# Two triangles of sliding-window scores merged into one matrix before the softmax and parted after the transpose

## The chip, the cores and the metric

The kernel runs on one core of a Trainium2 chip. The metric is the device time of one execution in microseconds; beside it stands a profile of one execution, in which times count from the first instruction. TensorE is PE in the rows (PEld are its weight loads), VectorE is DVE, ScalarE is ACT, GpSimd is POOL, and SP issues most of the transfers.

## The reference, cut to what matters

The reference is one inference step of a decoder layer with two branches: a retention branch and a sliding-window attention branch with learned sinks, 16 query heads in 4 groups of 4, head size 64, window 128. Only the second branch for the prompt (1024 tokens, 8 blocks of 128) is touched:

```python
i = arange(128)[:, None]; j = arange(256)[None, :]
d = i + 128 - j
band = (d >= 0) & (d < 128)             # keys of the block before, and of this one
s = q k^T * HD**-0.5, -inf outside band # 128 queries x 256 keys
p = softmax(concat([s, sink]))[..., :-1]
o = p v
```

For query i, the allowed keys of the block before are those with j > i, and those of its own block are those with j <= i. The two sets are complementary triangles of a 128x128 square. Block 0 has no block before it.

## The kernel before

Work is in three phases; all of the change lies in the first, which projects the normalised tokens and runs both branches. Every fp32 product is done with operands split into a high part (rounded to the fast matmul type, by ScalarE) and a low part (the rest, by a subtract on VectorE or GpSimd): `copy_hi_lo` at L138. The weights are split by `load_unit`, L151 to L170, ScalarE for the high part (L168) and GpSimd for the low part (L169), up to six units at a time and two units ahead of their use.

Phase one goes through eight groups: four heads of retention, then four key groups of the sliding window (4 query heads each). Each group goes over eight tiles of 128 tokens. A tile of the sliding window (`swa_tile`) has five parts, and the loop in `groups` interleaves those of neighbouring tiles with blocks of gate and merge projections (`gate_block`, `mg_block`: 24 matmuls of 344 columns each):

1. projection of 384 columns (24 matmuls), rotary and norm, in which GpSimd raises the mean squares to the power -0.5 (`rstd`, L147);
2. transposes of queries and keys (L512, L513) and their splits;
3. scores: for each of four heads two matmuls of 256 columns (L532, L533) into PSUM; then VectorE adds the band mask, scales by the query's norm and takes the row maximum in one instruction per head (L536), writing 128x256 to `s`; then `softmax_tail`: exponentials on ScalarE (L486), and a scaling by 1/sum per head on VectorE (L491);
4. for both key blocks: four transposes of `s` on TensorE into one PSUM tile (L546), high part on ScalarE, low part on VectorE (L549, both in the helper's lines L139 and L140);
5. for both key blocks two matmuls of 512 columns with the split values (L556, L557).

Tiles with t = 0 have one key block only. The decode rows (`swa_rows`) use the same `softmax_tail` with one head and 128 keys.

The order of instructions on each engine is not the program's: a planner (L984, `schedule_with_timeline_sim=True`) walks the program with durations of its own and, for each engine, writes down the instructions as they become ready, earlier program parts first. At run time each engine keeps to that order and waits on semaphores. Buffers are limited: three accumulators in PSUM for projections, two tiles for transposes (`ptr`), two for scores (`psc`), one for the product with the values (`pav`).

Of the kernel before, what the change touches and what calls it, by code (L numbers as in the profile page):

```python
# [8 lines left out]

F32 = mybir.dt.float32  # L10
F32R = mybir.dt.float32r
AF = mybir.ActivationFunctionType
ALU = mybir.AluOpType
AX = mybir.AxisListType
# [3 lines left out]
P = 128  # L18
# [9 lines left out]
SH, KVH, G, HD = 16, 4, 4, 64  # L28
WIN = 128
# [3 lines left out]
NEG = -1e30  # L33
# [38 lines left out]
def shape_constants():  # L72
    c, s = rope_tables(DK)
    out = {}
    cols = SEQ + NS
    ct = np.concatenate([c[:cols].T, c[:cols].T], 0)
    st = np.concatenate([s[:cols].T, -s[:cols].T], 0)
    out["c_ropeT"] = np.stack([ct, st], 1)
    tm = np.concatenate([c, s], 1).reshape(NT + 1, P, 128)
    tm[NT] *= DK ** -0.5  # L80
    out["c_ropeK"] = tm.transpose(1, 0, 2)
    c2, s2 = rope_tables(HD)
    tm = np.concatenate([c2, s2], 1).reshape(NT + 1, P, HD)
    out["c_ropeS"] = tm.transpose(1, 0, 2)
    lg = log_decay()
    m = np.arange(P)[:, None]
    n = np.arange(P)[None, :]
    sc = DK ** -0.5
    out["c_maskT"] = np.stack([(n >= m) * np.exp(-(m + 1.0) * lg[h]) * sc for h in range(RH)], 1)
    i = np.arange(P)[:, None]  # L90
    j = np.arange(2 * P)[None, :]
    d = i + P - j
    out["c_band"] = np.where((d >= 0) & (d < WIN), 0.0, NEG)
    misc = np.zeros((P, 8 + 8 + 64 + 128 + 8))
    for h in range(RH):
        misc[:, h] = np.exp((np.arange(P) + 1.0) * lg[h])
        misc[:, 4 + h] = np.exp((P - 1.0 - np.arange(P)) * lg[h]) * sc
    for r in (0, 32, 64):
        misc[r : r + 8, 8:16] = np.eye(8)
    misc[:, 16:80] = np.eye(8).reshape(1, 64)  # L100
    z = np.zeros((2, HD, NS // 2, NS, G))
    for b in range(NS):
        z[b % 2, :, b // 2, b, :] = 1.0
    misc[:, 80:208] = z.reshape(P, 128)
    for r in range(NS * G):
        misc[r, 208 + r // G] = 1.0
    out["c_misc"] = misc
    return {k: np.ascontiguousarray(v.astype(np.float32)) for k, v in out.items()}
# [14 lines left out]
class Body:  # L123
# [27 lines left out]
    def load_unit(self, spec):  # L151
# [3 lines left out]
        raw = self.t(self.wp, [P, D], "wraw", bufs=RAW)  # L155
        hi = self.t(self.wp, [P, D], "whi", F32R, bufs=self.wbufs)
        lo = self.t(self.wp, [P, D], "wlo", F32R, bufs=self.wbufs)
        view = lambda x: x[:, : nk * width].rearrange("p (k c) -> p k c", k=nk)
# [81 lines left out]
    def norm_h(self, t):  # L240
# [16 lines left out]
        else:  # L257
            junk = self.t(self.ap, [NS, NS, DK], "zk", F32R, bufs=1)[:]
        ss = self.t(self.sm, [P, 1], "ss", bufs=4)
# [82 lines left out]
    def ret_tile(self, h, t, units, qT, st, oT):  # L342
# [4 lines left out]
        self.rope_k(kr[:], acc[:, :DK], t)  # L347
        vhi = self.t(self.ap, [P, DV], "vhi", F32R, bufs=3)
        vlo = self.t(self.ap, [P, DV], "vlo", F32R, bufs=3)
# [124 lines left out]
        nc.vector.tensor_scalar(out=kd[:p], in0=kr[:p].broadcast_to([p, 2, HD]), scalar1=rs[:, 4:5], scalar2=None, op0=ALU.mult)  # L474
        return qr, kd, rs

    def softmax_tail(self, s, mx, nsink, sink, p, nh, nk):
        nc = self.nc
        ng = self.t(self.sm, [P, 4], "ng", bufs=2)
        ds = self.t(self.sm, [P, 4], "ds", bufs=2)  # L480
        l = self.t(self.sm, [P, 4], "l", bufs=2)
        r = self.t(self.sm, [P, 4], "r", bufs=2)
        nc.vector.scalar_tensor_tensor(out=ng[:p, :nh], in0=mx, scalar=-1.0, in1=nsink, op0=ALU.mult, op1=ALU.min)  # L483
        nc.vector.tensor_tensor(out=ds[:p, :nh], in0=sink, in1=ng[:p, :nh], op=ALU.add)
        for j in range(nh):
            nc.scalar.activation(out=s[:p, j, :nk], in_=s[:p, j, :nk], func=AF.Exp, bias=ng[:p, j : j + 1], accum_out=l[:p, j : j + 1])  # L486
        nc.scalar.activation(out=ds[:p, :nh], in_=ds[:p, :nh], func=AF.Exp)
        nc.vector.tensor_tensor(out=l[:p, :nh], in0=l[:p, :nh], in1=ds[:p, :nh], op=ALU.add)
        nc.vector.reciprocal(out=r[:p, :nh], in_=l[:p, :nh])
        for j in range(nh):  # L490
            nc.vector.tensor_scalar(out=s[:p, j, :nk], in0=s[:p, j, :nk], scalar1=r[:p, j : j + 1], scalar2=None, op0=ALU.mult)  # L491

    def swa_tile(self, g, t, units, st, oT):
        nc = self.nc
        acc = self.t(self.pacc, [P, 512], "acc")
        self.gemm_tok(acc[:, :384], units, self.hhi, self.hlo, t)
        qr, kd, rs = self.swa_rope(acc[:, :384], t)
# [12 lines left out]
        pt = self.t(self.ptr, [P, 4, P], "tr")  # L510
# [4 lines left out]
        for a in range(2):  # L515
            src = pt[a * HD : (a + 1) * HD, 0:2, :]
# [5 lines left out]
        yield  # L522
        k0 = (t - 1) * P if t else 0
        nk = 2 * P if t else P
        band = self.band[:, 2 * P - nk :]
        s = self.t(self.ap, [P, G, 2 * P], "s", bufs=2)
        mx = self.t(self.sm, [P, 4], "mx", bufs=2)
        for i in range(2):
            sc = self.t(self.psc, [P, 2, 256], "sc")
            for a in range(2):  # L530
                j = 2 * i + a
                nc.tensor.matmul(sc[:, a, :nk], qs[:, i, a, :], khi[:, k0 : k0 + nk], start=True, stop=False)  # L532
                nc.tensor.matmul(sc[:, a, :nk], qs[:, i, a, :], klo[:, k0 : k0 + nk], start=False, stop=True)  # L533
            for a in range(2):
                j = 2 * i + a
                nc.vector.tensor_tensor_reduce(  # L536
                    out=s[:, j, :nk], in0=sc[:, a, :nk], in1=band, scale=rs[:, j : j + 1], scalar=-3e38,
                    op0=ALU.add, op1=ALU.max, accum_out=mx[:, j : j + 1])
        self.softmax_tail(s, mx[:], self.nsink[:, G * g : G * g + G], self.sink[:, G * g : G * g + G], P, G, nk)
        yield  # L540
        nblk = nk // P
        pT = []
        for blk in range(nblk):
            pt = self.t(self.ptr, [P, 4, P], "tr")
            for j in range(G):
                nc.tensor.transpose(out=pt[:, j, :], in_=s[:, j, blk * P : (blk + 1) * P], identity=self.ident[:])  # L546
            hi = self.t(self.ap, [P, 512], "pThi", F32R, bufs=2)
            lo = self.t(self.ap, [P, 512], "pTlo", F32R, bufs=2)
            self.copy_hi_lo(hi[:], lo[:], pt[:].rearrange("p a b -> p (a b)"), nc.vector)  # L549
            pT.append((hi, lo))  # L550
        yield
        vs = [vprev, vv] if nblk == 2 else [vv]
        po = self.t(self.pav, [P, 512], "av")
# [11 lines left out]
    def swa_rows(self, g, units, oT):  # L565
        nc = self.nc
# [5 lines left out]
        qr, kd, rs = self.swa_rope(kv[:], NT, NS)  # L572
# [8 lines left out]
        pt = self.t(self.ptr, [P, 512], "tr")  # L581
# [5 lines left out]
        pt = self.t(self.ptr, [P, 512], "tr")  # L587
# [8 lines left out]
        R = NS * G  # L596
        sc = self.t(self.psc, [P, 512], "sc")
        for i in range(NS // 2):
            nc.tensor.matmul(sc[:R, :P], zq[:, i].rearrange("p a b -> p (a b)"), kcT[:, i * P : (i + 1) * P], start=(i == 0), stop=(i == NS // 2 - 1))
        s = self.t(self.ap, [R, 1, P], "srow", bufs=1)  # L600
        mx = self.t(self.sm, [P, 4], "mx", bufs=2)
        nc.vector.tensor_copy(out=s[:, 0, :], in_=sc[:R, :P])
        nc.vector.tensor_reduce(out=mx[:R, 0:1], in_=s[:, 0, :], axis=AX.X, op=ALU.max)
        self.softmax_tail(s, mx[:R, 0:1], self.nsinkr[:, g : g + 1], self.sinkr[:, g : g + 1], R, 1, P)
        yield
        pt = self.t(self.ptr, [P, 512], "tr")
        nc.tensor.transpose(out=pt[:, :R], in_=s[:, 0, :], identity=self.ident[:R, :R])
# [10 lines left out]
        pt = self.t(self.ptr, [P, 512], "tr")  # L618
# [226 lines left out]
    def swa_consts(self):  # L845
        nc, ap = self.nc, self.ap
        self.cK = self.t(ap, [P, NS, KVH * HD], "cK")
        self.cV = self.t(ap, [P, NS, KVH * HD], "cV")
        self.swa_tables()
        nc.sync.dma_start(out=self.rng[:], in_=self.i["ret_norm_g"][0].rearrange("h (i p) -> p (h i)", p=P))  # L850
        nc.vector.tensor_scalar(out=self.rng[:], in0=self.rng[:], scalar1=0.5, scalar2=None, op0=ALU.mult)
        self.band = self.t(ap, [P, 2 * P], "band")
        nc.sync.dma_start(out=self.band[:], in_=self.i["c_band"][:])
        self.sink = self.t(ap, [P, SH], "sink")
        nc.sync.dma_start(out=self.sink[:], in_=self.i["swa_sinks"][0:1, :].broadcast_to([P, SH]))
        self.nsink = self.t(ap, [P, SH], "nsink")
        nc.vector.tensor_scalar(out=self.nsink[:], in0=self.sink[:], scalar1=-1.0, scalar2=None, op0=ALU.mult)
        self.sinkr = self.t(ap, [NS * G, KVH], "sinkr")
        for b in range(NS):
            nc.sync.dma_start(out=self.sinkr[b * G : (b + 1) * G, :], in_=self.i["swa_sinks"][0].rearrange("(g j) -> j g", g=KVH))  # L860
        self.nsinkr = self.t(ap, [NS * G, KVH], "nsinkr")
        nc.vector.tensor_scalar(out=self.nsinkr[:], in0=self.sinkr[:], scalar1=-1.0, scalar2=None, op0=ALU.mult)
        for dst, name in ((self.cK, "cache_swa_k"), (self.cV, "cache_swa_v")):
            nc.sync.dma_start(out=dst[:], in_=self.i[name][0].rearrange("b k g d -> k b (g d)"))
# [123 lines left out]
```

## Time and profile before

| | |
|---|---|
| median of 3 runs | 1203.67 us (1202.83 to 1205.09) |
| profiled execution, its own time | 1204.67 us |
| its span, first to last instruction | 1202.9 us |
| mean granted clock of TensorE | 0.997 of full speed |
| busy: TensorE, VectorE, ScalarE, GpSimd | 1180.1, 671.3, 456.7, 355.4 us |

Matmuls overlap in their pipeline, so the duration of one is longer than the distance to the next; what one more matmul costs is read from the starts of neighbours. Idle time of an engine counts only if TensorE in the end waits for it.

### The profile page before, as it was taken

The numbers are of one execution on the slowest core, as the hardware profiler recorded it, in microseconds if no ns is written. First come the engines' busy times: TensorE is split into PE (matmuls) and PEld (weight loads), VectorE is DVE, ScalarE is ACT, GpSimd is POOL, SyncE is SP. The second block draws the span as 40 slices with busy tenths as digits, with TensorE's granted clock in tenths as the row PEclk, the third lists the DMA queues.
The fourth block names the chain that finished last, engine by engine and source line by source line (L and its number), as shares of the span: only waits on it lengthen the run. The fifth ranks groups of instructions, "written<-read, shape, count | busy, mean of one in ns | idle before, by whom it ended". The sixth has DMA issues, their size and how long they took to land.

```text
span 1202.9 us, 19501 instructions
## 1 busy us (share of the span) xinstructions
PE 1180.1 (98%) x7228; PEld 1114.3 (93%) x7228; DVE 671.3 (56%) x2018; ACT 456.7 (38%) x1158; POOL 355.4 (30%) x282
## 2 busy tenths in 40 slices
PE   6999999999999999999999999999999999999998
PEld 5899999999999999999999999999899999999876
DVE  5755545555544477777766777677754421565121
ACT  6543443334334245554454446444544310221010
POOL 5425016216225432422342224122532131221010
PEclk9999999999999999999999999999999999999999
DMA  9124115313113401310141013101526744554221
GB/s 324 51 72 118 55 42 162 112 42 108 51 61 101 139 32 57 109 37 19 44 135 37 8 56 110 55 7 37 172 65 241 230 149 143 166 161 138 78 89 71
DMA packets 125168, 116.71 MB, mean 97 GB/s; under 512 B 17480, under 2 KB 113224, under 8 KB 125040
## 3 DMA queue, kind: packets, MB, share of 16 engines
q1 hardware_dynamic: 118160, 106.99, 28.7%
q10 hardware_dynamic: 6912, 8.46, 2.0%
q8 instruction: 57, 0.93, 0.3%
q14 instruction: 39, 0.32, 0.1%
HBM read 85.05 MB, written 32.44 MB: 98 GB/s over the span
## 4 chain that ended last, share of the span: by engine, by line
PE 93%; DVE 4%; ACT 1%; DMA 1%; issue 1%; POOL 0%; SPq 0%; ACTq 0%
PE acc L212 16%; PE acc L213 16%; PE acc L214 16%; PE acc L223 10%; PE acc L224 10%; PE acc L222 9%; PE tr L546 2%; PE acc L233 1%; PE acc L232 1%; PE av L441 1%; PE sc L532 1%; PE sc L533 1%; PE av L557 1%; DVE s L491 1%; PE av L556 1%; PE tr L339 1%
## 5 line engine op out<-in xcount | busy, mean ns | idle before, releaser
L169 POOL TENSOR_TENSOR wlo<-wraw,whi 128x1024 fp32r<-128x1024 f32 (+1 forms) x92 | 204.9, 2236 | 335.5 <-ACT whi L168 250.1
L212 PE MATMUL acc<-hhi,whi 128*128 128x344 f32 x864 | 281.0, 325 | 0.6 <-ACT tg L298 0.6
L213 PE MATMUL acc<-hlo,whi 128*128 128x344 f32 x864 | 278.8, 323 | 0.0
L214 PE MATMUL acc<-hhi,wlo 128*128 128x344 f32 x864 | 278.3, 322 | 0.0
L222 PE MATMUL acc<-whi,hhi 128*128 128x384 f32 x512 | 175.1, 343 | 2.4 <-ACT hhi L139 1.2
L224 PE MATMUL acc<-whi,hlo 128*128 128x384 f32 x512 | 175.4, 343 | 0.0
L223 PE MATMUL acc<-wlo,hhi 128*128 128x384 f32 x512 | 175.3, 343 | 0.0
L212 PEld LDWEIGHTS acc<-hhi,whi 128*128 128x128 f32 x864 | 162.8, 188 | 2.3 <-ACT tg L298 0.9
L213 PEld LDWEIGHTS acc<-hlo,whi 128*128 128x128 f32 x864 | 162.5, 188 | 1.8 <-issue 1.0
L214 PEld LDWEIGHTS acc<-hhi,wlo 128*128 128x128 f32 x864 | 162.5, 188 | 1.4 <-issue 0.6
L147 POOL TENSOR_TENSOR rs<-ms,nhalf 128x1 f32<-128x1 f32 (+3 forms) x81 | 69.4, 858 | 298.3 <-DVE ms L146 294.1
L168 ACT ACTIVATE whi<-wraw 128x1024 fp32r<-128x1024 f32 (+1 forms) x92 | 90.2, 982 | 163.1 <-PE acc L213 104.5
L222 PEld LDWEIGHTS acc<-whi,hhi 128*128 128x128 f32 x512 | 97.2, 190 | 3.9 <-ACT hhi L139 1.6
L223 PEld LDWEIGHTS acc<-wlo,hhi 128*128 128x128 f32 x512 | 97.5, 190 | 1.5 <-issue 0.8
L224 PEld LDWEIGHTS acc<-whi,hlo 128*128 128x128 f32 x512 | 97.3, 190 | 0.5 <-DVE hlo L140 0.2
L486 ACT ACTIVATE s<-s,ng 128x256 f32<-128x256 f32 (+1 forms) x128 | 61.7, 484 | 27.3 <-DVE ng L483 27.2
L288 POOL TENSOR_TENSOR oT<-oT,tg 128x344 f32<-128x344 f32 x48 | 45.7, 954 | 84.3 <-DVE tg L286 61.6
L536 DVE CUSTOM_DVE_ANT_0 s<-sc,band,rs 128x256 f32<-128x256 f32 (+1 forms) x128 | 53.6, 460 | 17.9 <-PE sc L533 17.7
L139 ACT ACTIVATE pThi<-tr 128x512 fp32r<-128x512 f32 x60 | 35.2, 596 | 52.5 <-PE tr L546 52.1
L140 DVE TENSOR_TENSOR pTlo<-tr,pThi 128x512 fp32r<-128x512 f32 x60 | 41.0, 686 | 21.3 <-ACT pThi L139 20.9
L491 DVE TENSOR_SCALAR s<-s,r 128x256 f32<-128x256 f32 (+1 forms) x128 | 52.1, 468 | 0.7
L224 PE MATMUL acc<-whi,mlo 128*128 128x512 f32 x128 | 50.5, 395 | 0.0
(346 smaller groups left out, 2364.2 us busy)
## 6 DMA issues: line engine op xcount, KB each, us to landing
wraw<-in_w_in SPq DMA_DIRECT2D x36, 512.0 KB
d_t<-tg ACTq DMA_DIRECT2D x48, 172.0 KB
d_o<-oT SPq DMA_DIRECT2D x16, 516.0 KB
tt<-d_t SPq DMA_DIRECT2D x48, 172.0 KB
wraw<-in_w_in SPq DMA_DIRECT2D x32, 256.0 KB
st<-d_o SPq DMA_DIRECT2D x9, 516.0 KB
d_m<-tt SPq DMA_DIRECT2D x24, 172.0 KB
mm<-d_m SPq DMA_DIRECT2D x24, 172.0 KB
```

What stands on the lines that cost most here:

```text
L147: nc.gpsimd.tensor_tensor(out=rs[:p, :width], in0=ms[:p, :width], in1=self.nhalf[:p, :width], op=ALU.pow)
L168: nc.scalar.activation(out=hi[:, :f], in_=raw[:, :f], func=AF.Copy)
L169: nc.gpsimd.tensor_tensor(out=lo[:, :f], in0=raw[:, :f], in1=hi[:, :f].bitcast(F32), op=ALU.subtract)
L212: nc.tensor.matmul(ps, whi[:, k, :], hi[:, cs], start=(k == 0), stop=False)
L213: nc.tensor.matmul(ps, whi[:, k, :], lo[:, cs], start=False, stop=False)
L214: nc.tensor.matmul(ps, wlo[:, k, :], hi[:, cs], start=False, stop=(k == KT - 1))
L222: nc.tensor.matmul(ps, hi[:, k, a:b], whi[:, kk, :], start=(k == 0), stop=False)
L223: nc.tensor.matmul(ps, hi[:, k, a:b], wlo[:, kk, :], start=False, stop=False)
L224: nc.tensor.matmul(ps, lo[:, k, a:b], whi[:, kk, :], start=False, stop=(k == KT - 1))
L486: nc.scalar.activation(out=s[:p, j, :nk], in_=s[:p, j, :nk], func=AF.Exp, bias=ng[:p, j : j + 1], accum_out=l[:p, j : j + 1])
L491: nc.vector.tensor_scalar(out=s[:p, j, :nk], in0=s[:p, j, :nk], scalar1=r[:p, j : j + 1], scalar2=None, op0=ALU.mult)
L536: nc.vector.tensor_tensor_reduce(out=s[:, j, :nk], in0=sc[:, a, :nk], in1=band, scale=rs[:, j : j + 1], scalar=-3e38, op0=ALU.add, op1=ALU ...
```

## The change

The 256 score columns are merged into 128: where the key index is greater than the query index, the score of the block before is copied over that of the own block, in PSUM, by a predicated copy on VectorE (in tiles with t = 0 a constant -1e30 instead). Row maximum, exponentials, normalisation and transpose then run on one 128x128 matrix per head. The maximum is taken before the norm scale and multiplied with it afterwards; the exponentials read PSUM and apply the scale. The four scalings become one product with a broadcast operand. Behind the transpose and the split, for t > 0, GpSimd parts the matrix: two affine selects write copies of the high and low part that keep keys > query (for the values of the block before), and two more clear the same places in the originals, in place. The product with the values is unchanged. The mask constant becomes a 128x128 one of zeros and ones, and a 128x128 tile `neg` is filled once.

```diff
-    def softmax_tail(self, s, mx, nsink, sink, p, nh, nk):
+    def softmax_tail(self, s, src, scale, mx, nsink, sink, p, nh):
...
-            nc.scalar.activation(out=s[:p, j, :nk], in_=s[:p, j, :nk], func=AF.Exp, bias=ng[:p, j : j + 1], accum_out=l[:p, j : j + 1])
+            nc.scalar.activation(out=s[:p, j, :], in_=src[j], func=AF.Exp, bias=ng[:p, j : j + 1], scale=scale[j], accum_out=l[:p, j : j + 1])
...
-        for j in range(nh):
-            nc.vector.tensor_scalar(out=s[:p, j, :nk], in0=s[:p, j, :nk], scalar1=r[:p, j : j + 1], scalar2=None, op0=ALU.mult)
+        nc.vector.tensor_tensor(out=s[:p], in0=s[:p], in1=r[:p, :nh].unsqueeze(2).broadcast_to([p, nh, P]), op=ALU.mult)
...
-            for a in range(2):
-                j = 2 * i + a
-                nc.vector.tensor_tensor_reduce(
-                    out=s[:, j, :nk], in0=sc[:, a, :nk], in1=band, scale=rs[:, j : j + 1], scalar=-3e38,
-                    op0=ALU.add, op1=ALU.max, accum_out=mx[:, j : j + 1])
+            cur = sc[:, :, nk - P : nk]
+            nc.vector.copy_predicated(
+                out=cur, mask=two(self.after[:].bitcast(U32)), data=sc[:, :, 0:P] if t else two(self.neg[:]))
+            nc.vector.tensor_reduce(out=mx[:, 2 * i : 2 * i + 2], in_=cur, axis=AX.X, op=ALU.max)
+            scs += [sc[:, a, nk - P : nk] for a in range(2)]
+        nc.vector.tensor_tensor(out=mx[:], in0=mx[:], in1=rs[:, 0:G], op=ALU.mult)
...
-        for blk in range(nblk):
-            pt = self.t(self.ptr, [P, 4, P], "tr")
-            for j in range(G):
-                nc.tensor.transpose(out=pt[:, j, :], in_=s[:, j, blk * P : (blk + 1) * P], identity=self.ident[:])
-            hi = self.t(self.ap, [P, 512], "pThi", F32R, bufs=2)
-            lo = self.t(self.ap, [P, 512], "pTlo", F32R, bufs=2)
-            self.copy_hi_lo(hi[:], lo[:], pt[:].rearrange("p a b -> p (a b)"), nc.vector)
-            pT.append((hi, lo))
+        pt = self.t(self.ptr, [P, 4, P], "tr")
+        for j in range(G):
+            nc.tensor.transpose(out=pt[:, j, :], in_=s[:, j, :], identity=self.ident[:])
+        hi, lo = new("pThi"), new("pTlo")
+        self.copy_hi_lo(hi[:], lo[:], pt[:].rearrange("p a b -> p (a b)"), nc.vector)
+        pT = [(hi, lo)]
+        if t:
+            hp, lp = new("pHp"), new("pLp")
+            for dst, src, sign in ((hp, hi, 1), (lp, lo, 1), (hi, hi, -1), (lo, lo, -1)):
+                nc.gpsimd.affine_select(
+                    out=big(dst), in_=big(src).bitcast(F32), compare_op=ALU.is_ge, fill=0.0,
+                    base=-1 if sign > 0 else 0, pattern=[[0, G], [-sign, P]], channel_multiplier=sign)
+            hc, lc = hi, lo
+            pT = [(hp, lp), (hc, lc)]
```

The new helpers `two` (a broadcast over two heads), `big` (a view by heads) and `new` (a 128x512 tile; two buffers for `pThi` and `pTlo`, one for `pHp` and `pLp`) only shape operands.

## Rows read from the trace of the kernel before

**Rows 1.** Page, span and part one: busy us, share and instructions of each engine.
```profile
span 1202.9 us, 19501 instructions
...
PE 1180.1 (98%) x7228; PEld 1114.3 (93%) x7228; DVE 671.3 (56%) x2018; ACT 456.7 (38%) x1158; POOL 355.4 (30%) x282
```
**Rows 2.** Busy time by stretch, sliding-window stage; columns in the first line.
```profile
core 0: us, PE busy (x) PEld busy (x) DVE busy (x) ACT busy (x) POOL busy (x), PEclk, DMA share, GB/s
440.00:905.00 465.00, 462.18 (x2920) 439.77 (x2919) 336.15 (x1172) 230.34 (x645) 144.50 (x98) 1.00 0.21 62
```
**Rows 3.** Waits of TensorE, that stage: who, for whom, us in total, times, longest.
```profile
PE tr L546 <- DVE s L491: 2.7, 3, 1.8
```
**Rows 4.** Groups by shape, TensorE, that stage: busy us, mean ns | idle before.
```profile
L546 PE MATMUL tr<-ident,s 128*128 128x128 f32 x240 | 43.1, 274 | 2.8 <-DVE s L491 2.7
```
**Rows 5.** Chain that ended last, 470 to 473 us: start, us, what.
```profile
470.97 0.16 PE acc L212
...
471.45 0.44 PE tr L546 x4
```
**Rows 6.** Order in time, TensorE: start and us; four single transposes lie between.
```profile
467.29 0.32 PE L212 MATMUL acc<-hhi,whi 128*128 128x344 f32 x1
467.45 0.27 PE L546 MATMUL tr<-ident,s 128*128 128x128 f32 x1
...
468.52 0.32 PE L214 MATMUL acc<-hhi,wlo 128*128 128x344 f32 x1
```
**Rows 7.** Groups by shape, VectorE, that stage.
```profile
L491 DVE TENSOR_SCALAR s<-s,r 128x256 f32<-128x256 f32 x112 | 47.1, 481 | 0.6
L536 DVE CUSTOM_DVE_ANT_0 s<-sc,band,rs 128x256 f32<-128x256 f32 x108 | 46.9, 476 | 17.0 <-PE sc L533 16.9
L140 DVE TENSOR_TENSOR pTlo<-tr,pThi 128x512 fp32r<-128x512 f32 x60 | 41.0, 686 | 21.3 <-ACT pThi L139 20.9
...
L474 DVE TENSOR_SCALAR kd<-skr,rs 128x128 f32<-128x128 f32 x29 | 13.4, 463 | 2.8 <-POOL rs L147 2.0
...
L484 DVE TENSOR_TENSOR ds<-sink,ng 128x4 f32<-128x4 f32 x31 | 8.0, 257 | 0.7
```
**Rows 8.** Groups by shape, ScalarE, that stage.
```profile
L486 ACT ACTIVATE s<-s,ng 128x256 f32<-128x256 f32 x112 | 55.5, 498 | 23.4 <-DVE ng L483 23.2
L139 ACT ACTIVATE pThi<-tr 128x512 fp32r<-128x512 f32 x60 | 35.2, 596 | 52.5 <-PE tr L546 52.1
...
L486 ACT ACTIVATE s<-s,ng 128x128 f32<-128x128 f32 x12 | 4.7, 392 | 3.9 <-DVE ng L483 3.9
```
**Rows 9.** Groups by shape, GpSimd, whole span.
```profile
L169 POOL TENSOR_TENSOR wlo<-wraw,whi 128x768 fp32r<-128x768 f32 x32 | 61.1, 1919 | 40.4 <-ACT whi L168 32.0 <-PE acc L224 8.3
L288 POOL TENSOR_TENSOR oT<-oT,tg 128x344 f32<-128x344 f32 x48 | 45.7, 954 | 84.3 <-DVE tg L286 61.6 <-DVE oT L563 10.1 <-DVE l L488 4.6
L147 POOL TENSOR_TENSOR rs<-ms,nhalf 128x5 f32<-128x5 f32 x32 | 39.1, 1223 | 145.8 <-DVE ms L146 145.8
...
L589 POOL COPY kc<-cK 128x512 f32<-128x512 f32 x4 | 2.5, 618 | 8.2 <-DMA cK<-kd 8.2
...
masks.py:199 POOL TENSOR_SCALAR_AFFINE_SELECT ident<-ident 128x128 f32<-128x128 f32 x1 | 0.3, 288 | 0.0
...
L976 POOL MEMSET const-float32-0.0<- 128x1 f32 x1 | 0.1, 103 | 0.2 <-issue 0.2
```
**Rows 10.** Order in time, VectorE (two stretches) and GpSimd.
```profile
580.52 1.14 DVE L491 TENSOR_SCALAR s<-s,r 128x256 f32<-128x256 f32 x4
...
732.54 4.33 DVE L491 TENSOR_SCALAR s<-s,r 128x256 f32<-128x256 f32 x4
...
732.91 5.65 POOL L169 TENSOR_TENSOR wlo<-wraw,whi 128x768 fp32r<-128x768 f32 x3 [1.36 <-ACT whi L168]
```
**Rows 11.** Order in time, VectorE and TensorE: second subtract and its matmul, two tiles.
```profile
459.12 0.69 DVE L140 TENSOR_TENSOR pTlo<-tr,pThi 128x512 fp32r<-128x512 f32 x1
462.89 0.50 PE L557 MATMUL av<-pTlo,vv 128*128 128x512 f32 x1
...
633.90 0.69 DVE L140 TENSOR_TENSOR pTlo<-tr,pThi 128x512 fp32r<-128x512 f32 x1
637.98 0.39 PE L557 MATMUL av<-pTlo,vv 128*128 128x512 f32 x1
```
**Rows 12.** Instructions of the select's line; order in time, GpSimd, what follows it.
```profile
masks.py:199 POOLq MODIFY_POOL_CONFIG  x2: 8/8/8, 1.3 to 1.3; - x2
...
5.69 0.56 POOL L147 TENSOR_TENSOR rs<-ms,nhalf 128x1 f32<-128x1 f32 x1 [4.04 <-DVE ms L146]
```

More of the change, by code (lines that the diff above doesn't have):

```diff
@@ L11 @@
 F32R = mybir.dt.float32r
+U32 = mybir.dt.uint32
 AF = mybir.ActivationFunctionType
@@ L90, in shape_constants @@
     i = np.arange(P)[:, None]
-    j = np.arange(2 * P)[None, :]
-    d = i + P - j
-    out["c_band"] = np.where((d >= 0) & (d < WIN), 0.0, NEG)
+    j = np.arange(P)[None, :]
+    out["c_band"] = (j > i) * 1.0
     misc = np.zeros((P, 8 + 8 + 64 + 128 + 8))
@@ L524, in swa_tile @@
         nk = 2 * P if t else P
-        band = self.band[:, 2 * P - nk :]
-        s = self.t(self.ap, [P, G, 2 * P], "s", bufs=2)
+        s = self.t(self.ap, [P, G, P], "s", bufs=2)
         mx = self.t(self.sm, [P, 4], "mx", bufs=2)
+        two = lambda x: x.unsqueeze(1).broadcast_to([P, 2, P])
+        scs = []
         for i in range(2):
@@ L533, in swa_tile @@
                 nc.tensor.matmul(sc[:, a, :nk], qs[:, i, a, :], klo[:, k0 : k0 + nk], start=False, stop=True)
-            for a in range(2):
-                j = 2 * i + a
-                nc.vector.tensor_tensor_reduce(
-                    out=s[:, j, :nk], in0=sc[:, a, :nk], in1=band, scale=rs[:, j : j + 1], scalar=-3e38,
-                    op0=ALU.add, op1=ALU.max, accum_out=mx[:, j : j + 1])
-        self.softmax_tail(s, mx[:], self.nsink[:, G * g : G * g + G], self.sink[:, G * g : G * g + G], P, G, nk)
@@ L540, in swa_tile @@
-        yield
-        nblk = nk // P
-        pT = []
-        for blk in range(nblk):
-            pt = self.t(self.ptr, [P, 4, P], "tr")
-            for j in range(G):
-                nc.tensor.transpose(out=pt[:, j, :], in_=s[:, j, blk * P : (blk + 1) * P], identity=self.ident[:])
-            hi = self.t(self.ap, [P, 512], "pThi", F32R, bufs=2)
-            lo = self.t(self.ap, [P, 512], "pTlo", F32R, bufs=2)
-            self.copy_hi_lo(hi[:], lo[:], pt[:].rearrange("p a b -> p (a b)"), nc.vector)
-            pT.append((hi, lo))
+            cur = sc[:, :, nk - P : nk]
@@ new lines, in swa_tile @@
+            nc.vector.copy_predicated(
[3 more added lines that the diff above has]
+        nc.vector.tensor_tensor(out=mx[:], in0=mx[:], in1=rs[:, 0:G], op=ALU.mult)
+        self.softmax_tail(s, scs, [rs[:, j : j + 1] for j in range(G)], mx[:], self.nsink[:, G * g : G * g + G], self.sink[:, G * g : G * g + G], P, G)
@@ new lines, in swa_tile @@
+        yield
+        pt = self.t(self.ptr, [P, 4, P], "tr")
+        for j in range(G):
+            nc.tensor.transpose(out=pt[:, j, :], in_=s[:, j, :], identity=self.ident[:])
+        big = lambda x: x[:].rearrange("p (j n) -> p j n", j=G)
+        new = lambda nm: self.t(self.ap, [P, 512], nm, F32R, bufs=2 if "T" in nm else 1)
+        hi, lo = new("pThi"), new("pTlo")
[9 more added lines that the diff above has]
+            pT = [(hp, lp), (hc, lc)]
@@ L551, in swa_tile @@
+        nblk = len(pT)
         yield
@@ L603, in swa_rows @@
         nc.vector.tensor_reduce(out=mx[:R, 0:1], in_=s[:, 0, :], axis=AX.X, op=ALU.max)
-        self.softmax_tail(s, mx[:R, 0:1], self.nsinkr[:, g : g + 1], self.sinkr[:, g : g + 1], R, 1, P)
+        self.softmax_tail(s, [s[:, 0, :]], [1.0], mx[:R, 0:1], self.nsinkr[:, g : g + 1], self.sinkr[:, g : g + 1], R, 1)
         yield
@@ L851, in swa_consts @@
         nc.vector.tensor_scalar(out=self.rng[:], in0=self.rng[:], scalar1=0.5, scalar2=None, op0=ALU.mult)
-        self.band = self.t(ap, [P, 2 * P], "band")
-        nc.sync.dma_start(out=self.band[:], in_=self.i["c_band"][:])
+        self.after = self.t(ap, [P, P], "band")
+        nc.sync.dma_start(out=self.after[:], in_=self.i["c_band"][:])
+        self.neg = self.t(ap, [P, P], "neg")
+        nc.gpsimd.memset(self.neg[:], NEG)
         self.sink = self.t(ap, [P, SH], "sink")
```

## Prediction

> **What bounds the kernel.** I read the page's first part, then the stretch of the sliding-window tiles, then the costliest groups there, the chain of waits, and the order in time of single tiles. TensorE is busy for 1180.1 of 1202.9 us [rows 1]: whatever leaves its queue shortens the run, and whatever makes it wait lengthens it. All that the change touches lies from about 440 to 905 us. There TensorE is busy 462.2 of 465 us, VectorE 336.2, ScalarE 230.3, GpSimd 144.5, and the granted clock is 1.00 (the 2.4 GHz level) [rows 2]. So in this stretch no other engine is a bound by its load. Their work matters only where a result reaches TensorE later than its turn in the written order; that happens three times over the whole stage, 2.7 us in all, and each time it is the normalised scores that come late [rows 3].
>
> **TensorE: what leaves.** A tile with t > 0 now transposes four 128x128 blocks in place of eight: 4 x 7 = 28 tiles x 4 = 112 of the 240 transposes [rows 4] go. What is one worth? The mean of 274 ns is no price, since matmuls overlap. Four in a row take 0.44 us of the chain, 0.11 us each, where a 344-column matmul takes 0.16 [rows 5]. Where they stand singly among such matmuls the answer is nearly the same: from 467.29 to 468.52 us TensorE starts five matmuls with four transposes between them in 1.23 us [rows 6]; five times 0.16 is 0.80, which leaves 0.43 us for the four. So 112 x 0.11 = **12.3 us**. The score matmuls (256 columns) and the four 512-column matmuls with the values stay as they are: the parted matrix is again two operands, hi and lo. The merge saves no TensorE time there.
>
> **VectorE, per tile.** Out go four fused add-and-max (476 ns), four scalings (481 ns) and one 512-column subtract (686 ns) [rows 7]: 1.90 + 1.92 + 0.69 = 4.5 us. In come two predicated copies of 2x128 columns in PSUM, two max reductions over 2x128, one 128x4 product, and one 512-column product with a broadcast operand. No predicated copy stands in the trace. I price it like the fused operation, which also reads PSUM and SBUF for 256 columns: 0.48 us; bounds 0.26 (an operation on four columns) and 0.69 (512 columns). The reduction, over as many columns from PSUM, gets the same price and bounds; the small product 0.26, the large one 0.69 [rows 7]. Sum 4 x 0.48 + 0.26 + 0.69 = 2.9 us (2.0 to 3.7), so VectorE loses about 1.6 us per tile (0.8 to 2.5), some 45 of its 336 us. On the path that is worth nothing but the three late scalings. They also turn into one instruction in place of four, so I expect those 2.7 us to shrink.
>
> **ScalarE, per tile.** Four exponentials go from 256 to 128 columns, 498 to 392 ns, and one 596 ns copy goes [rows 8]: 0.43 + 0.60 = 1.0 us less, at least 0.6 if reading PSUM eats the first term. It is hidden either way; without cover it would be a gain.
>
> **GpSimd, per tile.** Four affine selects of 128x512 come in for the 28 tiles. The trace has one select, 128x128 in 288 ns, beside a 128x1 fill at 103 ns [rows 9]. Taking the fill as the fixed part, 0.10 + 4 x 0.185 = 0.84 us. Bounds: below, the 128x512 copy at 0.62; above, a two-input operation, between 954 ns for 344 columns and 1919 for 768, so 1.34 for 512 [rows 9]. I take 0.84, since the row is the same instruction: 3.4 us per tile (2.5 to 5.3), 94 us in the stage (69 to 150). GpSimd goes from 144 to some 239 of 465 us, 63% at the worst. Behind the selects in its queue stand the low halves of the weights, the gate products and the 1.2 us powers [rows 9]. The weights are fetched two units ahead, and GpSimd is no releaser in the waits of TensorE that I read; the powers feed the key scaling, before which VectorE stands idle for 2.0 us in all now [rows 7]; that will grow a little.
>
> **The new wait.** The matmuls with the values used to follow the second subtract; now they follow the last select. Single tiles show what is spare. The subtract that starts at 459.12 ends at 459.81, and its matmul stands at 462.89; the one of 633.90 ends at 634.59, its matmul stands at 637.98 [rows 11]. TensorE sat in neither gap: it did gate and projection matmuls, because the planner writes the order by its own durations and takes this chain for about 3.1 us longer than it is. The same planner will place these matmuls behind what it thinks the selects last. So they come late only if its figure for four selects is over 3.1 us too short. If it granted them nothing, 3.4 - 3.1 = 0.3 us per tile, 8 us in all, would be lost; if it grants half, nothing. There is work to put between: a tile's share of the stage is 465 / 32 = 14.5 us, mostly matmuls that do not need this result, and the last tiles still have the gate and merge blocks ahead of them. Without that cover the last select's 3.4 us per tile would cost 95 us.
>
> **The shared port.** In the trace the four scalings of one tile take 4.33 us, just while three weight subtracts run on GpSimd from 732.91 on [rows 10]. Undisturbed, four take 1.14 us (from 580.52 us [rows 10]). So a VectorE operation that uses two SBUF reads waits out a GpSimd operation. The Trainium skill says so too (SBUF — State Buffer, "SBUF: two separate sides"): the pair of ports that both engines share is an exclusive lock held for a whole instruction, so 112 selects would be 112 more holders. From rows: selects fill 3.4 of 14.5 us, 23%; some seven VectorE operations of a tile have their operands in SBUF; each meets a select with that chance and then waits half of 0.84 us: 7 x 0.23 x 0.42 = 0.7 us per tile, less than the 1.6 us that VectorE gains. I take it as covered.
>
> **Smaller edits.** The scores stay in PSUM until the exponentials have read them, longer than before; two such buffers serve one tile, and the next tile asks for them a tile's 14.5 us later. The mask's load is halved, one fill of 128x128 comes in on GpSimd, and both lie ahead of the stage. The decode rows run the same tail with one scaling each: nothing.
>
> **Sum.** The profiled execution is 1204.7 us, 1.0 above the median of 1203.7. Against its own time: -12.3 us of transposes, and a balance of waits that I set at +1 (2.7 us may go, some 3 to 4 may come): 1193.4 us. Against the median, 1192.4; I give 1192.
>
> **Rivals.**
> First, part of the gain is given back: the planner grants the selects little, or late powers and scalings (port) reach TensorE. The rows give up to 0.3 us per tile from the first, 8 us: 1196 to 1201.
> Second, the gain does not come: the score buffers, held longer, make the next scores wait, or the order turns out with other holes. It takes 12.3 / 28 = 0.44 us per tile. For it: two buffers only. Against: 14.5 us between uses. 1201 to 1206.
> Third, slower: the selects are so late that TensorE stands in front of the matmuls with the values. It decides once they are late by more than 0.44 us per tile; with no grant by the planner that is a select of over (3.1 + 0.44) / 4 = 0.89 us, close to my 0.84; with 1.34 us it costs (5.3 - 3.1) x 28 = 62 us, 1253 us. For it: the GpSimd power already lets VectorE wait, so the planner is less generous on that engine; and GpSimd runs in order, with subtracts of 1.9 us ahead. Against: a grant of nothing is unlikely, and a subtract is in the planner's order as well. 1206 to 1253.
> Fourth, each return to selects loads code. The only select of the trace comes with two MODIFY_POOL_CONFIG of 8 ns, and the next other compute operation starts 4.04 us later, put down to VectorE [rows 12]. Were that the price of a switch, a tile would be late by 3.4 + 4.0 - 3.1 = 4.3 us: 120 us, 1312 us. Against: no idle time stands ahead of the select itself (0.0 in its group [rows 9]). The Trainium skill (GPSIMD Engine Reference, "Instruction dispatch") has the first call of freshly loaded code pay about 6 us with nothing shown in the profile; by that figure, an estimate, a tile would be 6.3 us late and the run some 1368 us long, and the 0.0 ahead of the select does not agree with it.
>
> **Chances.** Transposes go and waits stay small (1187 to 1196): 0.63. Part given back (1196 to 1201): 0.15. No gain: 0.08. Slower by late selects: 0.12; by loading: 0.02. Two thousandths of this time, 2.4 us, is what can be told from no change, so faster holds 0.78, same 0.08, slower 0.14. The range from 1187 to 1203 takes the first two and a part of the third, 0.8.
>
> **What the new profile would show.** TensorE with 128 transposes in this line and about 12 us less busy; the select at 0.6 to 1.3 us; GpSimd at about half of the stage; VectorE and ScalarE down; the stage nearly 453 us long. Wrong, if the waits of TensorE name GpSimd or the value matmuls' operands with more than a few us, or if a configuration stands ahead of each group of selects with a hole behind it.

## The result and the profile after

The changed kernel takes 1189.42 us (median of 4, 1186.77 to 1191.22) against 1204.06 for the kernel before (median of 4, one more than ahead of the prediction); the ratio is 0.9871, interval [0.9848, 0.9893]. That is 14.6 us less; 1192 was forecast, 1187 to 1203 as the range.

The first lines of the page after: span, and busy us by engine, to be held against [rows 1].

```profile
span 1188.1 us, 19187 instructions
...
PE 1166.6 (98%) x7116; PEld 1103.2 (93%) x7116; DVE 644.3 (54%) x1798; ACT 438.7 (37%) x1130; POOL 429.0 (36%) x395
```

The span is 14.8 us shorter. TensorE's busy time fell by 13.5 us and its instructions by 112; span less busy, its idle time, went from 22.8 to 21.5. The stage of the sliding window, the columns of [rows 2]:

```profile
440.00:905.00 465.00, 463.41 (x2908) 443.44 (x2907) 315.52 (x969) 219.30 (x626) 221.86 (x211) 1.00 0.24 73
```

GpSimd has 77 us more in this window, VectorE 21 less, ScalarE 11 less; the clock is the same. (The window holds the whole stage after the change, but before it ends 15 us short of the next phase; over the whole span the differences are 73.6, 27.0 and 18.0 us.) The waits of TensorE from 430 us to the first matmul of the next phase (904.9 us; 920.0 before), as in [rows 3]:

```profile
PE acc L212 <- ACT tg L298: 1.4, 1, 1.4
PE sc L532 <- ACT kThi L139: 0.2, 1, 0.2
```

The late scalings are gone, and no wait names GpSimd. Groups by shape in that stage, TensorE's transposes and VectorE's new operations (busy us, mean ns | idle before):

```profile
L544 PE MATMUL tr<-ident,s 128*128 128x128 f32 x128 | 19.2, 272 | 0.0
```

```profile
L537 DVE TENSOR_REDUCE mx<-sc 128x2 f32<-128x256 f32 x62 | 24.8, 416 | 0.7
L535 DVE COPY_PREDICATED sc<-band,sc 128x256 f32<-128x256 uint32 x56 | 22.7, 423 | 9.9 <-PE sc L533 9.5
...
L490 DVE TENSOR_TENSOR s<-s,r 128x512 f32<-128x512 f32 x31 | 21.8, 705 | 0.5
L472 DVE TENSOR_TENSOR skr<-skr,su 128x64 f32<-128x64 f32 x29 | 12.2, 422 | 0.1
...
L539 DVE TENSOR_TENSOR mx<-mx,rs 128x4 f32<-128x4 f32 x31 | 10.3, 332 | 0.7
```

And the selects, groups by shape on GpSimd:

```profile
L553 POOL TENSOR_SCALAR_AFFINE_SELECT pTlo<-pTlo 128x512 fp32r<-128x512 f32 x28 | 18.9, 673 | 0.0
L553 POOL TENSOR_SCALAR_AFFINE_SELECT pThi<-pThi 128x512 fp32r<-128x512 f32 x28 | 18.7, 669 | 0.0
L553 POOL TENSOR_SCALAR_AFFINE_SELECT pLp<-pTlo 128x512 fp32r<-128x512 f32 x28 | 18.1, 645 | 5.3 <-DVE pTlo L140 3.9 <-DVE l L488 0.7
L553 POOL TENSOR_SCALAR_AFFINE_SELECT pHp<-pThi 128x512 fp32r<-128x512 f32 x28 | 17.9, 640 | 32.1 <-ACT pThi L139 31.9
```

A select takes 0.64 to 0.67 us, nearer to the copy of as many columns (0.62) than to my 0.84. One tile in order of time, GpSimd and then TensorE:

```profile
479.27 0.64 POOL L553 TENSOR_SCALAR_AFFINE_SELECT pHp<-pThi 128x512 fp32r<-128x512 f32 x1 [6.18 <-ACT pThi L139]
479.99 0.64 POOL L553 TENSOR_SCALAR_AFFINE_SELECT pLp<-pTlo 128x512 fp32r<-128x512 f32 x1
480.58 0.64 POOL L553 TENSOR_SCALAR_AFFINE_SELECT pThi<-pThi 128x512 fp32r<-128x512 f32 x1
481.16 0.64 POOL L553 TENSOR_SCALAR_AFFINE_SELECT pTlo<-pTlo 128x512 fp32r<-128x512 f32 x1
```

```profile
484.50 0.39 PE L564 MATMUL av<-pThi,vv 128*128 128x512 f32 x1
485.20 0.39 PE L565 MATMUL av<-pTlo,vv 128*128 128x512 f32 x1
```

The last select ends at 481.80, its matmul stands at 485.20: 3.4 us to spare, where the second subtract had 3.1 and 3.4 in [rows 11]. Over all 28 tiles this distance is 1.7 to 4.6 us, 3.4 on average. So the planner's order leaves the selects their time and keeps the same distance.

### The profile page after: what moved, and what is told of

The parts are those of the page before. It is cut to its first block, busy times and chain, and to the rows that moved or that the text cites. A ratio compares the mean times of both kernels' runs of the same rounds, so it can differ in the third digit from the quotient of the medians.

```text
span 1188.1 us, 19187 instructions
## 1 busy us (share of the span) xinstructions
PE 1166.6 (98%) x7116; PEld 1103.2 (93%) x7116; DVE 644.3 (54%) x1798; ACT 438.7 (37%) x1130; POOL 429.0 (36%) x395
## 4 chain that ended last, share of the span: by engine, by line
PE 92%; DMA 2%; DVE 2%; issue 1%; ACT 1%; POOL 1%; SPq 0%; ACTq 0%; POOLq 0%
PE acc L212 16%; PE acc L213 16%; PE acc L214 16%; PE acc L224 10%; PE acc L223 10%; PE acc L222 10%; PE acc L233 1%; PE acc L232 1%; PE sc L532 1%; PE av L441 1%; PE sc L533 1%; PE av L564 1%; PE av L565 1%; PE tr L544 1%; DMA oT<-d_o 1%
## 5 line engine op out<-in xcount | busy, mean ns | idle before, releaser
L288 POOL TENSOR_TENSOR oT<-oT,tg 128x344 f32<-128x344 f32 x48 | 48.3, 1007 | 63.1 <-DVE tg L286 58.6
L486 ACT ACTIVATE s<-sc,ng,rs 128x128 f32<-128x128 f32 x128 | 57.0, 456 | 17.4 <-DVE ng L483 17.3
L223 PE MATMUL acc<-wlo,mhi 128*128 128x512 f32 x128 | 50.3, 393 | 0.0
L222 PE MATMUL acc<-whi,mhi 128*128 128x512 f32 x128 | 50.1, 393 | 0.0
L965 DVE TENSOR_TENSOR x<-acc,x 128x512 f32<-128x512 f32 x16 | 11.0, 690 | 68.7 <-PE acc L224 68.7
L286 DVE SCALAR_TENSOR_TENSOR tg<-tg,acc 128x344 f32<-128x344 f32 x48 | 24.5, 511 | 35.7 <-ACT tg L285 35.5
```

Source lines behind the costliest of these rows:

```text
L222: nc.tensor.matmul(ps, hi[:, k, a:b], whi[:, kk, :], start=(k == 0), stop=False)
L223: nc.tensor.matmul(ps, hi[:, k, a:b], wlo[:, kk, :], start=False, stop=False)
L286: nc.vector.scalar_tensor_tensor(out=tg[:], in0=tg[:], scalar=1.0, in1=ps[:, :BL], op0=ALU.add, op1=ALU.mult)
L288: nc.gpsimd.tensor_tensor(out=sl, in0=sl, in1=tg[:], op=ALU.mult)
L486: nc.scalar.activation(out=s[:p, j, :], in_=src[j], func=AF.Exp, bias=ng[:p, j : j + 1], scale=scale[j], accum_out=l[:p, j : j + 1])
```

## The experiments

The account above leaves open whether the transposes alone are the gain, and what the other engines' share is. All twelve runs are in the order of their sections, each with the median of 4 to 12 executions. Each ratio is to executions of the kernel before that were taken beside that run (their medians are 1203.96 to 1205.58 us), so a difference of two medians and one of two ratios can disagree by about a microsecond. "Idle" is span less busy of TensorE in the profiled execution.

| kernel | transposes of `s` | median us | ratio to before | interval | TensorE busy | idle |
|---|---|---|---|---|---|---|
| before | 240 | 1204.1 | | | 1180.1 | 22.8 |
| changed | 128 | 1189.4 | 0.9871 | 0.9848 to 0.9893 | 1166.6 | 21.5 |
| 1 changed, transposes twice | 240 | 1197.2 | 0.9939 | 0.9928 to 0.9951 | 1176.7 | 19.9 |
| 2 before, half the transposes | 128 | 1200.2 | 0.9964 | 0.9951 to 0.9978 | 1171.6 | 27.0 |
| 3 changed, no selects | 128 | 1190.4 | 0.9876 | 0.9859 to 0.9893 | 1166.5 | 22.7 |
| 4 changed, selects twice | 128 | 1193.6 | 0.9907 | 0.9894 to 0.9920 | 1168.2 | 23.0 |
| 5 changed, VectorE masks | 128 | 1218.4 | 1.0108 | 1.0092 to 1.0125 | 1172.4 | 41.1 |
| 6 changed, four scalings | 128 | 1192.4 | 0.9903 | 0.9889 to 0.9917 | 1165.6 | 24.5 |
| 7 before, one scaling | 240 | 1198.9 | 0.9951 | 0.9938 to 0.9964 | 1177.7 | 20.9 |
| 8 changed, split twice | 128 | 1190.2 | 0.9881 | 0.9867 to 0.9896 | 1164.8 | 23.0 |
| 9 before, half and one scaling | 128 | 1197.0 | 0.9932 | 0.9915 to 0.9949 | 1167.0 | 26.6 |
| 10 changed, twice and four scalings | 240 | 1204.2 | 1.0002 | 0.9989 to 1.0014 | 1176.6 | 25.0 |
| 11 changed, maximum in halves | 128 | 1194.9 | 0.9912 | 0.9895 to 0.9929 | 1166.4 | 26.7 |
| 12 changed, other order of selects | 128 | 1199.4 | 0.9950 | 0.9932 to 0.9967 | 1168.2 | 28.7 |

**1. Every transpose twice.**

```diff
+        for _ in range(2 if t else 1):
             for j in range(G):
                 nc.tensor.transpose(out=pt[:, j, :], in_=s[:, j, :], identity=self.ident[:])
```

> The changed kernel, in which each of the 112 remaining transposes of tiles with t > 0 is done twice into the same PSUM place; nothing else is added. Theory A (the gain is the 112 transposes that left TensorE's queue, 0.11 to 0.125 us each): 12.3 to 14 us above the changed kernel's 1189.4, so 1202 to 1203.5, ratio to the kernel before 0.998 to 1.000. Theory B (the gain comes from the lighter VectorE and ScalarE, TensorE had room for transposes): within 3 us of 1189.4, ratio 0.988 to 0.990. Theory C (the selects are partly late and eat some of the gain): like A for this run.

7.7 us above the changed kernel: between the theories. TensorE's own work came back as priced, in the chain of waits eight in a row:

```profile
451.61 0.87 PE tr L545 x8
```

that is 0.11 us each again, and its busy time rose by 10.1 us. But its idle time fell by 1.6: a TensorE with more to do can reach late results later, which fits but is not shown by this run alone. Some 7 us of the gain stayed although all 240 transposes were there, which theory A had not allowed for.

**2. The kernel before with half the transposes.**

```diff
-            pt = self.t(self.ptr, [P, 4, P], "tr")
-            for j in range(G):
-                nc.tensor.transpose(...)
+            if blk == 0:
+                pt = self.t(self.ptr, [P, 4, P], "tr")
+                for j in range(G):
+                    nc.tensor.transpose(...)
```

> The kernel before, without the four transposes of the second key block in tiles with t > 0; both blocks' high and low parts are taken from the first block's transposes, so the second block's weights are left out, and all work of VectorE, ScalarE and the value matmuls stays. Theory A: 12.3 to 14 us below the kernel before, ratio 0.9885 to 0.990, and the waits for late scalings (2.7 us) stay. Theory B: ratio 0.997 to 1.000.

Only some 4 us faster, just outside theory B's range, whose lower end lies in the interval. Busy time fell by 8.5, idle time rose by 4.2. The waits of TensorE in the stage:

```profile
PE tr L547 <- DVE s L491: 6.3, 6, 2.0
PE acc L212 <- ACT tg L298: 1.3, 1, 1.3
```

The wait for late scalings, 2.7 us in [rows 3], is now 6.3. So theory A fails for the time; of TensorE's own work it has the direction, 8.5 us of 12.3, with a stretch of slower clock in between (last section).

**3 and 4. No selects, and selects twice.** Run 3 puts `pT = [(hi, lo), (hi, lo)]` in place of the four selects; run 4 writes each twice:

```diff
-            for dst, src, sign in ((hp, hi, 1), (lp, lo, 1), (hi, hi, -1), (lo, lo, -1)):
+            for dst, src, sign in ((hp, hi, 1), (lp, lo, 1), (hp, hi, 1), (lp, lo, 1), (hi, hi, -1), (lo, lo, -1), (hi, hi, -1), (lo, lo, -1)):
```

> The changed kernel without the four affine selects: the unparted matrix goes to both value matmuls, so the parting is left out. Theory A: the selects are hidden, within 2 us of the changed kernel, ratio 0.986 to 0.989. Theory C: 4 to 8 us faster than the changed kernel, ratio 0.980 to 0.984. Theory B: a little faster through a free port, 1 to 3 us.

> The changed kernel with every select done twice, eight per tile with t > 0, some 72 us more GpSimd work. Theory A: still hidden behind the planner's order, within 2 us of the changed kernel, ratio 0.986 to 0.989. Theory C: the value matmuls stand 2.6 us later per tile and TensorE waits, 10 to 70 us slower than the changed kernel, ratio over 0.995.

Without selects nothing is gained (intervals overlap wholly), so theory C falls: they are hidden. With twice as many the kernel is some 4 us slower, more than A's 2 and far less than C's range. Runs 11 and 12 move as much or more with next to no work of their own, so the 4 us cannot be put down to the selects; the largest single new wait of TensorE there is 2.6 us in front of the next phase's first matmul, not at a value matmul.

**5. Parting by mask products on VectorE.**

```diff
-                nc.gpsimd.affine_select(...)
+                m = self.part[sign][:].unsqueeze(1).broadcast_to([P, G, P])
+                nc.vector.tensor_tensor(out=big(dst), in0=big(src).bitcast(F32), in1=m, op=ALU.mult)
```

> The changed kernel with the parting done by four VectorE products with 0/1 masks of 128x512 in place of the four GpSimd selects: about 2.8 us more VectorE and 2.6 us less GpSimd per tile with t > 0. Theory D (what TensorE keeps of the saved transposes depends on how late VectorE's softmax chain runs): VectorE goes back to or over its load before, waits of TensorE grow, 3 to 12 us above the changed kernel, ratio 0.990 to 0.998. Theory A (only TensorE's own queue counts, other engines are hidden): within 2 us of the changed kernel, ratio 0.985 to 0.989.

29 us above the changed kernel and 13 above the one before: theory D's direction, over twice its size. Waits of TensorE in the stage (430 to 930 us):

```profile
PE av L563 <- DVE rbig L621: 3.5, 1, 3.5
PE tr L544 <- DVE s L490: 3.1, 2, 1.5
PE av L564 <- DVE pLp L554: 3.1, 3, 1.1
PE av L563 <- DVE pHp L554: 2.9, 2, 1.5
PE av L563 <- DVE pThi L554: 1.5, 1, 1.5
...
```

VectorE is busy for 381 of the 465 us from 440 us on, 82%, against 72% in [rows 2], and its results come late at several places. The same parting work cost nothing that could be seen on GpSimd (run 3), and with it on VectorE the kernel is 29 us slower, about three times the largest shift that a mere change of order brings (run 12).

**6 and 7. Four scalings or one, in both kernels.** Run 6 has a loop of four `tensor_scalar` of 128 columns in the changed kernel; run 7 has the broadcast product in the kernel before:

```diff
-        for j in range(nh):
-            nc.vector.tensor_scalar(out=s[:p, j, :nk], in0=s[:p, j, :nk], scalar1=r[:p, j : j + 1], ...)
+        nc.vector.tensor_tensor(out=s[:p, :, :nk], in0=s[:p, :, :nk], in1=r[:p, :nh].unsqueeze(2).broadcast_to([p, nh, nk]), op=ALU.mult)
```

> The changed kernel with four scalings of 128 columns in place of the one broadcast product. Theory D1 (within theory D: the late results are those of the four scalings, each of which can be held by a GpSimd operation): the waits for late scores return, 2 to 4 us above the changed kernel, ratio 0.989 to 0.991. Theory D2 (within theory D: it is the length of the whole chain and the load of VectorE that count, not the number of scalings): within 1.5 us, ratio 0.986 to 0.9885. Theory A: within 2 us as well.

> The kernel before with one broadcast product over 4x256 columns in place of the four scalings; nothing else is changed. Theory D1: the 3 us of waits for late scalings go, 2 to 4 us faster, ratio 0.9965 to 0.9985. Theory D2 and theory A: within 2 us of the kernel before, ratio 0.998 to 1.002, since the one product over 1024 columns lasts as long as four undisturbed scalings.

By the times as D1 said, and more in run 7: 3.0 us slower (3.9 by the ratios) and 5.8 us faster. The waits for the scaled scores, run 6 and then run 7:

```profile
PE tr L545 <- DVE s L491: 4.2, 4, 2.0
```

```profile
PE tr L545 <- DVE s L490: 1.2, 1, 1.2
```

In run 6 they are back, in four places. In run 7 they shrank from 2.7 us to 1.2 and did not go, so only 1.5 of the 5.8 us is traced to them; the rest is no larger than what a mere change of order moves in runs 11 and 12.

**8. Copy and subtract behind the transposes twice** (`for _ in range(2 if t else 1)` ahead of each).

> The changed kernel with the ScalarE copy and the VectorE subtract behind the transposes each done twice in tiles with t > 0, as many as before the change: 0.6 us of ScalarE and 0.69 us of VectorE more per tile. Theory D2: waits of TensorE grow, 2 to 6 us above the changed kernel, ratio 0.989 to 0.993. Theory D1 and theory A: within 2 us, ratio 0.986 to 0.989.

Within a microsecond of the changed kernel: the second split that the change removed shows no worth on the path, as forecast, and D2 falls in this form.

**9 and 10. Transposes and scalings together.** Run 9 is runs 2 and 7 in one; run 10 is runs 1 and 6 in one.

> The kernel before with both of two parts: the second key block's transposes left out (its weights are the first block's, as in the run with half the transposes) and one broadcast product in place of the four scalings. Theory E (the gain is the transposes' 12.3 us plus the late scalings; the transposes alone could not be kept because the scalings ran late): the two together bring more than their sum of 3.8 + 5.8, some 14 to 17 us, ratio 0.986 to 0.9885. Rival F (the two parts just add and the shorter columns bring the rest): 9.6 us, ratio 0.991 to 0.993.

> The changed kernel with both undone: every transpose of tiles with t > 0 twice, and four scalings in place of the one product. Theory E: the whole gain goes, 12 to 16 us above the changed kernel, ratio 0.997 to 1.001. Rival F (the parts add): 7.7 + 3.0 = 10.7 us above it, ratio 0.995 to 0.997, the remaining 4 us being what the lighter ScalarE and VectorE bring by themselves.

Run 10 gives theory E's number: with these two undone the whole gain is gone. Run 9 does not: 7 to 8 us in place of 14 to 17, less even than the sum in rival F; busy time is 1167.0, as in the changed kernel, but idle time is 26.6, with waits for scores and for a subtract:

```profile
PE tr L546 <- DVE s L490: 2.7, 1, 2.7
PE av L557 <- DVE pTlo L140: 2.3, 2, 2.0
```

So one scaling can come as late as four, and E fits the changed kernel and not the one before; neither theory covers both.

**11 and 12. The same work in another order.** Run 11 multiplies the maximum by halves inside the loop; run 12 only exchanges two selects:

```diff
-            for dst, src, sign in ((hp, hi, 1), (lp, lo, 1), (hi, hi, -1), (lo, lo, -1)):
+            for dst, src, sign in ((hp, hi, 1), (hi, hi, -1), (lp, lo, 1), (lo, lo, -1)):
```

> The changed kernel with the product of maximum and norm scale done in two halves of two columns in place of one of four; 0.2 us more VectorE per tile and no other change, so that only the planner's order differs. All theories: within 1 us of the changed kernel by the work itself; what it moves beyond that is the size of a chance change of order, which I put at up to 3 us, ratio 0.985 to 0.990.

> The changed kernel with the same four selects in another order (both of the high part first, then both of the low part): the same instructions, work and buffers, so only the order that the planner writes can differ. If a chance change of order is worth some 5 us (as the run with the halved product suggests), anything from 1186 to 1196 may come, ratio 0.985 to 0.993. If the halved product itself cost the 5.5 us there (0.2 us more on VectorE in the chain of every tile), this run lies within 1.5 us of the changed kernel, ratio 0.986 to 0.9885.

5.5 and 10.0 us slower than the changed kernel (4.9 and 9.5 by the ratios), more than what I had expected of such edits before run 11. The selects of run 12 last as long as before. Its three longest waits of TensorE from 430 to 930 us:

```profile
PE acc L212 <- ACT tg L298: 4.5, 1, 4.5
PE acc L212 <- DVE vv L140: 2.5, 1, 2.5
PE tr L544 <- DVE s L490: 2.0, 1, 2.0
```

They sit at two places; the last two at one, here by stretches of 5 us (PE is the first busy time, the clock stands behind POOL):

```profile
830.00:835.00 5.00, 5.00 (x34) 4.90 (x32) 3.14 (x10) 4.44 (x13) 5.00 (x5) 1.00 0.61 211
835.00:840.00 5.00, 1.18 (x7) 0.61 (x6) 4.94 (x8) 1.55 (x4) 4.97 (x3) 0.85 0.84 279
840.00:845.00 5.00, 4.35 (x15) 4.35 (x16) 1.91 (x7) 0.28 (x1) 2.46 (x3) 0.50 1.01 284
845.00:850.00 5.00, 5.00 (x35) 4.94 (x34) 2.09 (x4) 3.04 (x5) 1.60 (x1) 0.96 0.10 37
```

and there, in order of time, GpSimd and then VectorE:

```profile
834.24 2.37 POOL L169 TENSOR_TENSOR wlo<-wraw,whi 128x1024 fp32r<-128x1024 f32 x1
...
837.63 2.35 POOL L169 TENSOR_TENSOR wlo<-wraw,whi 128x1024 fp32r<-128x1024 f32 x1
```

```profile
834.73 2.43 DVE L490 TENSOR_TENSOR s<-s,r 128x512 f32<-128x512 f32 x1
...
838.16 1.84 DVE L146 TENSOR_SCALAR ms<-ss 128x5 f32<-128x5 f32 x1
```

The scaling that lasts 0.7 us elsewhere takes 2.43 and ends 0.55 after the weight subtract; the 5-column operation, 0.16 us undisturbed, ends with the next subtract. TensorE stands meanwhile (1.18 of 5 us busy), and runs the following stretch at half clock. The other place is around 910 us: the first matmul of the next phase waits 4.5 us for `tg`, which stands in ScalarE's queue behind an operation that had waited for a transfer:

```profile
910.92 1.15 ACT L881 ACTIVATE opA6h<-oT,rng 128x1032 fp32r<-128x1032 f32 x1 [5.17 <-DMA oT<-d_o]
```

## Why the prediction was right, and where by luck

**Transposes, 12.3 us.** Right, and a microsecond high. The four profiled executions with 240 transposes have TensorE busy for 1177.78 us on average (1176.6 to 1180.1); the seven with 128 and a mean clock of at least 0.996 (changed, 3, 4, 6, 8, 9, 11) for 1166.44 (1164.8 to 1168.2). That is 11.3 us, 0.10 per transpose, and run 1 shows 0.11 in the chain. The changed pair happens to show 13.5. So of the 14.8 us by which the span fell, 11.3 are the transposes; the other 2.2 us of busy time and 1.3 of idle time lie within the scatter of these runs, and no run gives them a cause.

**Waits, set at +1.** Small as forecast, but by the luck of this order. Idle time went from 22.8 to 21.5, but kernels with the same TensorE work and edits that add nothing or little on other engines (8, 11, 12) have 23.0, 26.7 and 28.7. With 128 transposes idle time is 21.5 to 28.7 (run 5 apart), with 240 it is 19.9 to 25.0. In three of the four pairs that differ in the transposes alone, the one with fewer of them waits longer: 21.5 against 19.9 (changed, 1), 27.0 against 22.8 (2, before), 26.6 against 20.9 (9, 7); in the fourth it is 24.5 against 25.0 (6, 10). What was kept of 11 to 12 us was 7.7, 3.8, 1.9 and 11.8 us, in this order (8.2, 4.3, 2.3 and 11.9 by the ratios). The forecast named the sources (late scores, planner) but not the spread: the two rewritten orders of runs 11 and 12 move the time by 5 and 10 us, one to two times the 4.5 us that I gave the likeliest case to either side, and both are slower than the changed kernel, whose own order is thus a good one. Run 12 lies at 1199.4 us, where the first rival (part of the gain given back, 1196 to 1201) was put.

**The late scalings.** Priced at the 2.7 us of the waits, and in the changed kernel they are gone. That one instruction in place of four is the reason is not shown: the times of runs 6 and 7 (3.0 and 5.8 us) go that way, but the one scaling is late too, for 1.2 us in run 7, 2.0 in run 12 and 2.7 in run 9. The mechanism that the forecast gave, a held port, is seen whole in run 12. The Trainium skill (SBUF — State Buffer, "SBUF: two separate sides") calls the shared ports an exclusive lock held for the instruction; the 2.43 us next to the 2.37 us subtract agree with it. The selects do it too, for less: of the 32 adds of 64 columns (L472) in the changed kernel, four beside a select last 0.64 to 0.65 us, three beside a weight subtract 1.85 to 2.04, the others 0.21 to 0.23; no wait of TensorE came from them. VectorE is busy for 634.0 us without selects (run 3), for 644.3 with them and for 650.1 in run 12, so they held it for some 10 to 16 us, where the forecast has 0.7 us in each of 28 tiles, 20 us.

**VectorE "worth nothing but the late scalings".** True for the split (run 8), and not to be widened: with 82% of the stage in place of 68 TensorE waits for it at many places (run 5). VectorE's busy time fell by 27.0 us, where the forecast has 45 less the port's 20. The price of the predicated copy, 0.48, measured 0.42; the reduction 0.42; the small product 0.33 for 0.26.

**Selects.** 0.84 us forecast, 0.64 to 0.67 measured. Hidden, as forecast (run 3). The slower rival fell with the planner's grant: 3.4 us of distance on average, about what [rows 11] had. The loading rival fell: no configuration stands ahead of any of the 112 selects, and no idle time ahead of the third and fourth of a tile; ahead of the first two GpSimd waits for ScalarE's and VectorE's results.

**Left open.** In the kernel before, halving the transposes and merging the scalings gave 7 us and not 14 (run 9). What brings the other 7, the shorter columns or merely the changed kernel's good order, these runs do not tell, since edits of no weight moved the time as much.

## What to carry to other kernels

When one engine is busy for 98% and a planner writes its order, count what leaves that engine's queue for the likeliest time, and expect that part of it can come back as waits: in three of four pairs here idle time rose as busy time fell. A range below the spread of two neutral rewrites is too narrow, and a difference below that spread is no evidence for a cause. Work to be added belongs on the engine with the longest distance to the bound: the same parting cost nothing visible on GpSimd, and the kernel with it on VectorE, which was at 68%, is 29 us slower. Short VectorE operations on the path are worth watching: a 5-column one, 0.16 us undisturbed, took 1.84 us beside a GpSimd subtract in run 12.

## What was not expected of the hardware

A pause of TensorE can cost more than its own length. In run 12 it was busy for 1.18 of the 5 us from 835 on, and in the next 5 us the granted clock was 0.50, the level of 1.2 GHz; then 0.96. The chain of waits has its 344-column matmuls there at 0.29 us in place of 0.16 [rows 5]; some 14 of them make 14 x 0.13 = 1.8 us, an estimate, on top of the 4.5 us of waiting:

```profile
841.31 0.29 PE acc L213
841.59 0.29 PE acc L214
```

The same is seen in run 2, where TensorE is busy for 4.02 and 3.75 us of the two stretches from 835 and 840 us and the clock of the second is 0.78, and in run 6, where 2.8 of the 4.2 us of waits for late scalings lie between 830 and 845 us:

```profile
835.00:840.00 5.00, 2.36 (x9) 2.16 (x10) 4.94 (x11) 0.98 (x2) 2.84 (x2) 0.70 1.02 349
840.00:845.00 5.00, 5.00 (x23) 5.00 (x22) 3.65 (x12) 2.63 (x4) 3.69 (x4) 0.62 0.78 201
```

The changed kernel, whose longest wait in the stage is 1.4 us, keeps 1.00 over it.
